# Moving the transposes of the next superblock's x into the first matmul, storing second-level results by whole rows, and pinning the order of matmuls and copies

## The chip, the cores and the metric

One core of one Trainium2 chip. The metric is the device time of one execution in microseconds (us).

## The reference

```python
x:  8 x 1024 x 1024 float32      w1: 1024 x 4096      w2: 4096 x 1024
h = x @ w1
h = 0.5 * h * (1 + np.tanh(np.sqrt(2 / np.pi) * (h + 0.044715 * h ** 3)))
return (h @ w2).astype(np.float32)
```

## The kernel before

The kernel works through eight superblocks (0 to 7) of 1024 rows of x. Each has a first matmul (x times w1, then the activation into `g`) and a second matmul (`g` times w2). Both use seven products of half-size blocks in place of eight (Strassen's scheme). In superblocks 2 to 7 some products of the second matmul are themselves split into seven smaller ones, with matmuls of 256 columns. These are the "inner" products, or the second level: 1, 2, 3, 6 and 7 in superblocks 3 to 7, and 2, 6 and 7 in superblock 2. The order of the products is 4, 1, 2, 3, 5, 6, 7. Superblocks 0 and 1 run code that the change does not touch.

Weights, operands and half results share one pool of 26 buffers named `u`. All loads, and the transposing DMAs, are issued by SP in one queue; casting and accumulating DMAs are issued by POOL.

```python
    up = ctx.enter_context(tc.tile_pool(name="up", bufs=26))
...
    def x_transpose(xb, dma):                    # 16 DMAs, x of one superblock, from the cast copy in DRAM
        blocks = x_blocks()                      # 4 buffers of the 26
        for b, t in blocks.items():
            a, k = int(b[0]) - 1, int(b[1]) - 1
            for j in range(KH):
                dma(t[:, j, :], xb[a * HT:(a + 1) * HT, (k * KH + j) * P:(k * KH + j + 1) * P],
                    transpose=True)
...
# first matmul, chunk c of 16: the next superblock's x is cast, late
            if 1 < sb < NSB - 1 and c in (8, 10, 12, 14):
                xb[0] = x_cast_paced(sb + 1, g["12"][:, c, :], c - 8, xb[0])
...
# an inner product: seven multiplies, each quarter of the result stored when it is done
            self.multiply(2, ab, False)
            ...
            self.done("11", c11)                 # store_quarter: rows of 256 float32, 1 KB
...
# second matmul
        def post5(q, ps):                        # product 5: first level, accumulates onto block 12
            store(sb, "12", q, copy(q, ps), accum_op=ADD)
            tt(u[q], u[q], ps, SUB, True)
            if not end:
                store(sb, "11", q, u[q])
...
        for m, after in zip(order, order[1:] + (None,)):
            if after is not None:
                load(after)                      # prefetch of the next product's weights
            if m == (1 if sb == 2 else 3):
                nxt[0] = next_x()                # the 16 transposes are issued here, on SP
...
```

The order of DVE's tensor operations in the second matmul is pinned to program order (`pin=True`). Matmuls and ACT's copies are placed by a scheduler when the kernel is built, and it interleaves neighbouring products.

Of the kernel before, what the change touches and what calls it, by code (L numbers as in the profile page):

```python
# [14 lines left out]
P = 128  # L15
# [75 lines left out]
def kernel(  # L91
# [14 lines left out]
    SB = 1024  # L106
# [47 lines left out]

    def load_in_order(out, in_, **kw):
        return tc.keep_in_program_order(nc.sync.dma_start(out=out, in_=in_, **kw))  # L156

    def pool_copy(out, in_):
        pool_last[0] = nc.gpsimd.tensor_copy(out=out, in_=in_)  # L159
# [180 lines left out]
        mark = nc.gpsimd.tensor_copy(out=pace, in_=g_chunk[:, :2])  # L340
        return x_cast(s, mark, range(q * P, (q + 2) * P, P), xb)

    def x_transpose(xb, dma):
        blocks = x_blocks()
        for b, t in blocks.items():
            a, k = int(b[0]) - 1, int(b[1]) - 1
            for j in range(KH):
                dma(  # L348
                    t[:, j, :],
                    xb[a * HT:(a + 1) * HT, (k * KH + j) * P:(k * KH + j + 1) * P],  # L350
                    transpose=True,
                )
        return blocks
# [3 lines left out]
    def matmul1(xs, sb, quads):  # L357
# [26 lines left out]
        more = []  # L384
        xb = [None]
        early = {1: {}, 2: {}}

        def ahead(q, step):

# [24 lines left out]
        for c in range(NI):  # L414
            q, j = divmod(c, QC)
            if sb > 1:
                if c % 2 == 0:
                    quads += [StoredHalf(i) for i in range(len(quads), min(c // 2 + 3, NI // 2))]
                w = quads[c // 2], c
            else:  # L420
                if j == 0:
                    ahead(q + 1, 0)
                w = quads[q], c
            pb, qb = psum(), psum()
            product(pb, w, 4, True, False)
            v = temp()
            nc.scalar.copy(out=v, in_=pb)  # L427
            product(qb, w, 5, True, False)
            u = temp()
            tt(u, v, qb, SUB)  # L430
            if late is not None:
                finish(*late)
            rb = psum()
            product(rb, w, 1, True, False)
            s = temp()
            tt(s, u, rb, ADD)
            if sb == 0 and c < 2:
                for m in SUMS:
                    quads[0].sum(m, more[c], True)
            product(pb, w, 2, False, True)  # L440
            gelu("21", c, pb)
            s2 = temp()
            tt(s2, s, pb, SUB)
            product(qb, w, 3, False, False)
            gelu("12", c, qb)
            product(rb, w, 7, False, True)
            c11 = temp()
            tt(c11, u, rb, ADD)
            gelu("11", c, c11)
            late = (c, w, qb, s2)  # L450
            if sb < 2 and j:
                ahead(q + 1, j)
            if 1 < sb < NSB - 1 and c in (8, 10, 12, 14):
                xb[0] = x_cast_paced(sb + 1, g["12"][:, c, :], c - 8, xb[0])
            if sb > 1 and c >= NI - 4:
                m, b = EARLY[c - NI + 4]
                if m in FILL_2[sb == 2]["inner"]:
                    early[m][b] = unit(NI // 2, HT // 2)
                    gu, gv = (inner_block(g[t], b) for t in A_TERMS[m])
                    nc.gpsimd.tensor_tensor(out=early[m][b], in0=gu, in1=gv, op=SUB)  # L460
        finish(*late)
        return g, xb[0], early



# [2 lines left out]
        o0 = (int(b[1]) - 1) * OH  # L468
        return nc.gpsimd.dma_start(out=out2[r0:r0 + P, o0:o0 + OH], in_=src, **kw)

    def store_quarter(sb, o, b, src, queue=None, add=None):
        add = queue is None if add is None else add
        queue = queue or nc.gpsimd
        r0 = sb * SB + (int(o[0]) - 1) * HT + (int(b[0]) - 1) * HT // 2
        o0 = (int(o[1]) - 1) * OH + (int(b[1]) - 1) * OH // 2
        rows = out2[r0:r0 + HT // 2, o0:o0 + OH // 2].rearrange("(i p) n -> p i n", p=P)
        return queue.dma_start(out=rows, in_=src, **(dict(accum_op=ADD) if add else {}))  # L477

    def matmul2_made(sb, g, keep_w1, xb):

# [135 lines left out]
                fill.pop(0)()  # L616
        while fill:
            fill.pop(0)()
        return at["last"], xs, [quad]

    def split_jobs(m, pieces):
        t = {}
# [32 lines left out]
    class Inner:  # L655


        def __init__(self, m, g, done=lambda b, t: None, base=None, x=()):
            self.m, self.done, self.base = m, done, base
            self.u, self.v = (None if b is None else g[b] for b in A_TERMS[m])  # L660
            self.x, self.s, self.y = dict(x), {}, {}
            if self.v is None:
                self.x = {b: inner_block(self.u, b) for b in BLOCKS}
# [16 lines left out]
        def multiply(self, j, bank, first):  # L680
            t = self.x[S_TERMS[j]] if j in S_TERMS else next(
                self.s[n] for n in S_SUMS if S_SUMS[n][0] == j
            )
            for i in range(2):
                for c in range(NI // 2):
                    nc.tensor.matmul(  # L686
                        bank[:, i * OH // 2:(i + 1) * OH // 2],
                        lhsT=t[:, c, i * P:(i + 1) * P],
                        rhs=self.y[j][:, c, :],
                        start=(first and i == 0 and c == 0),  # L690
                        stop=(c == NI // 2 - 1),
                        skip_group_check=not first or i > 0,
                    )

        def steps(self, into):

# [4 lines left out]
            ab, bb, cb = psum(), psum(), psum()  # L701
            self.multiply(1, ab, True)
            v = temp()
            nc.scalar.copy(out=v, in_=ab)
            yield 1
            self.multiply(6, bb, True)
            tt(c12, pair(v), pair(bb), ADD, True)
# [2 lines left out]
            yield 2  # L710
            self.multiply(2, ab, False)
            if base is None:
                nc.scalar.copy(out=c11, in_=pair(ab))
            else:
                tt(c11, b11, pair(ab), ADD, True)
            self.done("11", c11)
            yield 3
            self.multiply(7, bb, False)
            tt(c21, pair(v), pair(bb), ADD, True)
# [3 lines left out]
            yield 4  # L723
            self.multiply(5, cb, True)
            tt(c22, c21 if base is None else c22, pair(cb), ADD, True)
            self.done("22", c22)
            yield 5
            self.multiply(4, ab, True)
            tt(c21, c21, pair(ab), SUB, True)
            self.done("21", c21)  # L730
            yield 6
            self.multiply(3, cb, False)
            tt(c12, c12, pair(cb), ADD, True)
            self.done("12", c12)
            yield 7

    def operand2(g, m, q, pin=False):
# [6 lines left out]
        tt(a, g[u][:, :, cols], g[v][:, :, cols], SUB, pin)  # L744
        return a

    def matmuls2(bank, a, pieces, first, cs=range(NI)):
        for c in cs:
            nc.tensor.matmul(  # L749
                bank,  # L750
                lhsT=a[:, c, :],
                rhs=pieces[c // QC][:, c % QC, :],
# [1 line left out]
                stop=(c == NI - 1),  # L754
                skip_group_check=not first,
            )

    def product2(g, m, pieces, banks, first, by_chunk=False):
        if first:
# [13 lines left out]
        tiles = [up.tile([P, 2, OH], F32, name="u") for _ in range(2)]  # L773
        return tiles, [tiles[q // 2][:, q % 2, :] for q in range(NQ)]

    def matmul2(sb, g, early, next_x):
        inner = FILL_2[sb == 2]["inner"]
        fill = FILL_2[sb == 2]["fill"]
        end = sb == NSB - 1
        ops, pieces, splits = {}, {}, {}  # L780
        u2, u = halves()
        into, rows = {}, {}
        nxt = [None]

        products = {
            1: Inner(1, g, x=early[1]),
            2: Inner(2, g, lambda b, t: store_quarter(sb, "21", b, t), x=early[2]),
            3: Inner(3, g, lambda b, t: store_quarter(sb, "12", b, t, add=False)),
            6: Inner(6, g, lambda b, t: store_quarter(sb, "22", b, t)),
            7: Inner(  # L790
                7, g,
                lambda b, t: store_quarter(sb, "11", b, t, nc.sync if end else None),
                u2 if end else None,
            ),
        }

        def copy(q, ps):
            t = temp()
            nc.scalar.copy(out=t, in_=ps)
            return t  # L800

        def post4(q, ps):
            nc.scalar.copy(out=u[q], in_=ps)  # L803
            store(sb, "21", q, u[q])

        def post1(q, ps):
            nc.scalar.copy(out=rows[1][q], in_=ps)

        def post3(q, ps):
            d = rows[1][q]  # L810
# [18 lines left out]
        def run(key):  # L829
            for job in fill.get(key, ()):  # L830
# [13 lines left out]
                elif kind in "de":  # L844
                    b = job[1:]
                    d = quarter(into[1], b)
                    tt(d, d, quarter(into[2 if kind == "d" else 3], b), SUB if kind == "d" else ADD, True)
                    if kind == "e":
                        store_quarter(sb, "22", b, d, add=False)
                elif nxt[0] is not None:  # L850
                    nxt[0].make(m, pin=True)

        order = (4, 1, 2, 3, 5, 6, 7)
        load(4)
# [1 line left out]
        for m, after in zip(order, order[1:] + (None,)):  # L856
            if after is not None:
                load(after)
            if m == (1 if sb == 2 else 3):
                nxt[0] = next_x()  # L860
            if m in inner or m == 1:
                into[m], rows[m] = halves()
            if m in inner:
# [3 lines left out]
            for q in range(NQ):  # L867
                ps = psum()
                a = ops.get((m, q))
                matmuls2(ps, operand2(g, m, q) if a is None else a, pieces[m], True)  # L870
                posts[m](q, ps)
                run((m, q))
        return nxt[0]

    idle = consts.tile([P, HT], DT, name="idle")
    nc.vector.memset(idle, 0.0)
# [3 lines left out]
    nc.scalar.activation(out=warm, in_=warm, func=GELU)  # L880
    xs, quads = x_first(), []
    for sb in range(NSB):
        g, xb, early = matmul1(xs, sb, quads)
        if sb < 2:
            xb = x_cast(sb + 1, quads[2].stored) if sb else None
            last, xs, quads = matmul2_made(sb, g, None if sb else quads[-1].keep_raw, xb)
            continue
        def next_x():
            return XOps(x_transpose(xb, nc.sync.dma_start)) if xb is not None else None

        xs = matmul2(sb, g, early, next_x)
        if xs is not None:
            quads = [StoredHalf(0)]


# [28 lines left out]
```

## Time and profile before

| | before |
|---|---|
| time, median of the first 3 runs | 1576.93 us (1576.26 to 1580.64) |
| span of the profiled run | 1578.6 us |
| PE busy | 1531.9 us, 97% |
| superblock 2 | 205.2 us |
| superblocks 3 to 6 | 189.5, 195.6, 192.8, 192.5 us |
| superblock 7, to the end of the last matmul | 190.5 us |

A superblock is measured in PE's timeline, from the first matmul of 512 columns of its first matmul to that of the next one. What it needs can be worked out from durations in the same timeline. Sixteen 512-column matmuls in a row start 0.216 us apart, sixteen 256-column ones take 1.75 us (0.1094 each). So superblocks 3 to 7 need 448 x 0.216 + 128 x 0.216 + 560 x 0.1094 = 185.7 us, and superblock 2, with fewer inner products, 448 x 0.216 + 256 x 0.216 + 336 x 0.1094 = 188.8 us (the recorded texts say 188.9).

From the page of the kernel before, the line of the engines (busy us, share of the span, instructions):

```profile
PE 1531.9 (97%) x8606; PEld 839.5 (53%) x8606; DVE 1066.9 (68%) x1354; ACT 486.2 (31%) x821; POOL 387.2 (25%) x434
```

From the list of who waited for whom, PE's largest waits (total us, times, longest):

```profile
PE ps L686 <- DVE u L146: 11.9, 5, 10.3
PE ps L686 <- DMA u<-in_d: 11.8, 11, 2.0
PE ps L686 <- ACT tmp L704: 4.3, 6, 0.7
PE ps L686 <- DVE gc L146: 3.3, 6, 1.4
PE ps L364 <- DMA u<-w_d: 3.3, 9, 0.5
```

PE is 97% busy, so everything that can be won is a wait of PE, and the waits are short and many. L686 is the inner products' matmul; `in_d` holds their weights.

Three stretches of superblock 4 (us, then busy time and instruction count of PE, PEld, DVE, ACT, POOL, then PE's clock, the busy share of the DMAs, GB/s). The first lies in the first matmul, the other two in the second:

```profile
852.00:858.00 6.00, 6.00 (x29) 2.74 (x28) 3.40 (x6) 2.88 (x6) 1.30 (x1) 1.00 0.01 3
...
942.00:948.00 6.00, 6.00 (x56) 5.37 (x57) 6.00 (x9) 0.58 (x1) 3.80 (x4) 1.00 1.28 131
948.00:954.00 6.00, 5.82 (x45) 4.24 (x44) 5.14 (x8) 0.00 (x0) 0.92 (x2) 1.00 1.45 128
```

SP's timeline (start, us, engine, line, operation, count) and PE's (the bracket is the idle time before, and what ended it) in the same superblock:

```profile
933.12 26.81 SPq L348 DMA_TRANSPOSE u<-xb  x16
960.03 18.34 SPq L668 DMA_DIRECT2D u<-in_d  x14
```

```profile
975.42 1.92 PE L686 MATMUL ps<-u,gc 128*128 128x256 f16 x16 [1.96 <-DMA u<-in_d]
...
991.99 3.65 PE L686 MATMUL ps<-u,gc 128*128 128x256 f16 x32 [1.07 <-DMA u<-in_d]
```

Read together: in the first matmul the DMAs stand nearly idle at 852 us. In the second their busy share is above 1 at 942 to 954 us and yet they move only about 130 GB/s, while the 16 transposes run there. The loads of `in_d` are issued after them, and PE's waits for them end 15 to 32 us later. The time from issue to landing of these 14 loads:

```profile
DMA to landing us min/median/max: 5.8/17.2/19.6
```

Superblock 2 has one long wait. The chain of waits there (start, us, what):

```profile
581.41 14.35 DMA out_dram<-u
...
596.99 1.23 DVE u L146
```

PE's timeline at its end:

```profile
598.27 3.53 PE L686 MATMUL ps<-u 128*128 128x256 f16 x16 [10.29 <-DVE u L146]
```

DVE waited for a buffer that a store had to empty, and the store took 14.35 us to land. The 16 matmuls after the gap take 3.53 us, where others take 1.91 us. The Trainium skill ("TensorE: Matmul & The Clock Gate", Part 1) says that PE falls to half its clock after about 3.4 us of idleness and needs about 3.4 us of work to come back. This wait agrees: the clock column is 1.00 from 588 to 590 us, 0.50 from 592 to 600 us, and 1.00 again from 602 us.

### The profile page before, as it was taken

Reading aid. Unit: us, or ns where it says so; the run is one execution under the profiler, and the core shown is the slowest. Engines: PE = TensorE matmul, PEld = TensorE weight load, DVE = VectorE, ACT = ScalarE, POOL = GpSimd, SP = SyncE. Lnnn points to the kernel's source line nnn. Section 1 sums busy time; section 2 is a strip of 40 time slices with the busy share of each in tenths; the row PEclk is TensorE's granted clock in tenths of the full one; section 3 lists DMA queues with packets and bytes.
Section 4 is the critical chain, followed back from the end, with each engine's and each line's share of the span. In section 5 each row is a group of like instructions: output and inputs, shape, how many; then the busy total and the mean of one; then the engine's idle time right before and its main releaser. Section 6 shows DMA issues by size and latency. Waiting matters only on the chain.

```text
span 1578.6 us, 22771 instructions
## 1 busy us (share of the span) xinstructions
PE 1531.9 (97%) x8606; PEld 839.5 (53%) x8606; DVE 1066.9 (68%) x1354; ACT 486.2 (31%) x821; POOL 387.2 (25%) x434
## 2 busy tenths in 40 slices
PE   9999999999999988999999998999999999999998
PEld 4444444444444545447754476544765448644486
DVE  6876867879656557555865668656686566855577
ACT  6654024400344112441124411344113431144311
POOL 2341011223121332130422213131131401404022
PEclk9999999999999998999999999999999999999999
DMA  9999976985947999569995799957999579993597
GB/s 321 338 339 337 260 244 226 307 262 214 386 145 205 269 360 274 203 168 319 277 328 199 210 270 297 338 169 217 260 313 333 164 222 247 334 342 116 200 312 196
DMA packets 222221, 415.19 MB, mean 263 GB/s; under 512 B 78240, under 2 KB 102816, under 8 KB 221216
## 3 DMA queue, kind: packets, MB, share of 16 engines
q1 hardware_dynamic: 178560, 307.29, 58.7%
q0 software_dynamic: 43552, 106.45, 27.0%
q8 instruction: 67, 1.10, 0.3%
q14 instruction: 42, 0.34, 0.1%
HBM read 304.09 MB, written 124.26 MB: 271 GB/s over the span
## 4 chain that ended last, share of the span: by engine, by line
PE 75%; DMA 14%; DVE 4%; issue 4%; SPq 1%; ACT 1%; POOL 1%; POOLq 0%; DVEq 0%
PE ps L364 46%; PE ps L749 20%; PE ps L686 9%; DMA u<-in_d 6%; DMA u<-w_d 3%; DMA out_dram<-u 3%; DVE u L146 3%; DMA gc<-in_w_dram 2%; DVE gc L146 1%; DMA in_d<-u 1%; SPq L156 1%; DMA out_dram<-tmp 1%; ACT u L803 0%; SPq L348 0%; POOL u L159 0%
## 5 line engine op out<-in xcount | busy, mean ns | idle before, releaser
L364 PE MATMUL ps<-u 128*128 128x512 f16 x3584 | 778.2, 380 | 6.8 <-DMA u<-w_d 3.3
L364 PEld LDWEIGHTS <-u 128*128 128x128 f16 x3584 | 349.1, 98 | 433.8 <-DMA u<-w_d 8.5
L146 DVE TENSOR_TENSOR tmp<-tmp,ps 128x512 f32<-128x512 f32 x528 | 362.2, 687 | 299.1 <-ACT tmp L427 113.5
L374 ACT ACTIVATE g<-tmp 128x512 f16<-128x512 f32 x256 | 161.2, 630 | 294.7 <-DVE tmp L146 294.6
L749 PE MATMUL ps<-u,gc 128*128 128x512 f16 x1088 | 237.4, 380 | 0.0
L146 DVE TENSOR_TENSOR u<-u 128x2048 f16<-128x2048 f16 (+3 forms) x245 | 219.0, 923 | 18.2 <-ACT u L319 12.2
L686 PE MATMUL ps<-u,gc 128*128 128x256 f16 x1792 | 210.8, 273 | 9.1 <-DMA u<-in_d 5.6
L686 PEld LDWEIGHTS <-gc 128*128 128x128 f16 x1792 | 174.1, 98 | 36.8 <-issue 9.0
L374 ACT ACTIVATE g<-ps 128x512 f16<-128x512 f32 x256 | 151.4, 596 | 91.6 <-PE ps L364 90.6
L749 PEld LDWEIGHTS <-gc 128*128 128x128 f16 x1088 | 106.4, 98 | 126.3
L477 POOL DMA_DIRECT2D out_dram<-u x108 | 111.5, 1033 | 246.6 <-DVE u L146 183.2
L460 POOL TENSOR_TENSOR u<-g,g 128x2048 f16<-128x2048 f16 x22 | 89.1, 4072 | 296.9 <-ACT g L374 296.9
L686 PE MATMUL ps<-u 128*128 128x256 f16 x1104 | 136.4, 275 | 23.4 <-DVE u L146 11.2
L749 PE MATMUL ps<-u,g 128*128 128x512 f16 x704 | 154.2, 380 | 1.7 <-DMA u<-w_d 1.7
L686 PEld LDWEIGHTS <-u 128*128 128x128 f16 x1104 | 107.8, 98 | 43.8 <-DVE u L146 17.0
L749 PEld LDWEIGHTS <-g 128*128 128x128 f16 x704 | 68.9, 98 | 83.9 <-issue 1.5
L146 DVE TENSOR_TENSOR u<-tmp,ps 128x512 f32<-128x512 f32 x56 | 38.4, 686 | 109.4 <-PE ps L686 72.0
L146 DVE TENSOR_TENSOR u<-u,ps 128x512 f32<-128x512 f32 x129 | 88.1, 683 | 28.6 <-PE ps L749 17.1
L146 DVE TENSOR_TENSOR u<-g,g 128x2048 f16<-128x2048 f16 x70 | 83.5, 1220 | 19.6 <-DMA out_dram<-u 11.1
L427 ACT COPY tmp<-ps 128x512 f32<-128x512 f32 x128 | 72.9, 569 | 73.8 <-PE ps L364 73.6
L146 DVE TENSOR_TENSOR tmp<-ps,tmp 128x512 f32<-128x512 f32 x128 | 88.4, 691 | 6.4 <-PE ps L364 1.6
L146 DVE TENSOR_TENSOR gc<-g,g 128x2048 f16<-128x2048 f16 x68 | 82.3, 1219 | 3.0 <-PE ps L749 1.6
(43 smaller groups left out, 547.1 us busy)
## 6 DMA issues: line engine op xcount, KB each, us to landing
u<-in_d SPq DMA_DIRECT2D x196, 512.0 KB, 7.8
u<-w_d SPq DMA_DIRECT2D x240, 256.0 KB, 5.4
out_dram<-u POOLq DMA_DIRECT2D x164, 256.0 KB, 8.2
u<-raw_d SPq DMA_DIRECT2D x56, 512.0 KB, 7.1
gc<-in_w_dram SPq DMA_DIRECT2D x48, 512.0 KB, 6.1
u<-raw_d SPq DMA_DIRECT2D x96, 256.0 KB, 5.4
raw_d<-u SPq DMA_DIRECT2D x32, 512.0 KB, 9.8
w_d<-u POOLq DMA_DIRECT2D x32, 512.0 KB, 4.3
```

What stands on the lines that cost most here:

```text
L146: i = nc.vector.tensor_tensor(out=out, in0=in0, in1=in1, op=op)
L156: return tc.keep_in_program_order(nc.sync.dma_start(out=out, in_=in_, **kw))
L364: nc.tensor.matmul(bank, lhsT=ops[:, k, :], rhs=xs[m][:, k, :], start=(first and k == 0), stop=(k == KH - 1), skip_group_check=not first,)
L374: gelu_last[0] = nc.scalar.activation(out=g[b][:, c, :], in_=src, func=GELU)
L427: nc.scalar.copy(out=v, in_=pb)
L460: nc.gpsimd.tensor_tensor(out=early[m][b], in0=gu, in1=gv, op=SUB)
L477: return queue.dma_start(out=rows, in_=src, **(dict(accum_op=ADD) if add else {}))
L686: nc.tensor.matmul(bank[:, i * OH // 2:(i + 1) * OH // 2], lhsT=t[:, c, i * P:(i + 1) * P], rhs=self.y[j][:, c, :], start=(first and i == ...
L749: nc.tensor.matmul(bank, lhsT=a[:, c, :], rhs=pieces[c // QC][:, c % QC, :], start=(first and c == 0), stop=(c == NI - 1), skip_group_chec ...
```

## The change

The intent is to move the traffic for the next superblock's x out of the second matmul, to make the stores' rows longer, and to keep the products in the order in which they were written.

```diff
-            if 1 < sb < NSB - 1 and c in (8, 10, 12, 14):
-                xb[0] = x_cast_paced(sb + 1, g["12"][:, c, :], c - 8, xb[0])
+            if 1 < sb < NSB - 1:
+                if c in (1, 3, 5, 7):
+                    xb[0] = x_cast_paced(sb + 1, g["12"][:, c, :], c - 1, xb[0])
+                if c == 9:
+                    blocks = x_blocks()
+                if c > 8 and c % 2:
+                    x_transpose(xb[0], load_in_order, blocks, range((c - 9) // 2, (c - 7) // 2))
...
-            if m == (1 if sb == 2 else 3):
-                nxt[0] = next_x()
...
+    def store_rows(sb, o, a, src, **kw):
+        r0 = sb * SB + (int(o[0]) - 1) * HT + a * HT // 2
+        o0 = (int(o[1]) - 1) * OH
+        rows = out2[r0:r0 + HT // 2, o0:o0 + OH].rearrange("(i p) n -> p i n", p=P)
+        return nc.gpsimd.dma_start(out=rows, in_=src, **kw)
...
-            3: Inner(3, g, lambda b, t: store_quarter(sb, "12", b, t, add=False)),
+            3: Inner(3, g, out("12")),           # out: store_rows, called when both quarters of a row are done
...
+    def act_copy(out, in_):
+        tc.keep_in_program_order(nc.scalar.copy(out=out, in_=in_))
...
-                    nc.tensor.matmul(             # inner products; likewise in matmuls2
+                    tc.keep_in_program_order(nc.tensor.matmul(
```

The three parts are called X (early casts and transposes of x), R (rows of 2 KB) and P (pins) from here on.

More of the change, by code (lines that the diff above doesn't have):

```diff
@@ L341, in x_cast_paced, with x_transpose @@
         return x_cast(s, mark, range(q * P, (q + 2) * P, P), xb)
-    def x_transpose(xb, dma):
-        blocks = x_blocks()
-        for b, t in blocks.items():
+    def x_transpose(xb, dma, blocks=None, which=range(4)):
+        blocks = blocks or x_blocks()
+        for b, t in [list(blocks.items())[i] for i in which]:
             a, k = int(b[0]) - 1, int(b[1]) - 1
@@ L386, in matmul1 @@
         early = {1: {}, 2: {}}
+        blocks = None
         def ahead(q, step):
@@ L461, in matmul1 @@
         finish(*late)
-        return g, xb[0], early
+        return g, early, None if blocks is None else XOps(blocks)
     def store(sb, b, q, src, **kw):
@@ L469, in store, with store_quarter @@
         return nc.gpsimd.dma_start(out=out2[r0:r0 + P, o0:o0 + OH], in_=src, **kw)
-    def store_quarter(sb, o, b, src, queue=None, add=None):
-        add = queue is None if add is None else add
-        queue = queue or nc.gpsimd
+    def store_quarter(sb, o, b, src):
         r0 = sb * SB + (int(o[0]) - 1) * HT + (int(b[0]) - 1) * HT // 2
@@ L476, in store_quarter @@
         rows = out2[r0:r0 + HT // 2, o0:o0 + OH // 2].rearrange("(i p) n -> p i n", p=P)
-        return queue.dma_start(out=rows, in_=src, **(dict(accum_op=ADD) if add else {}))
+        return nc.sync.dma_start(out=rows, in_=src)
+    def store_rows(sb, o, a, src, **kw):
[3 more added lines that the diff above has]
+        return nc.gpsimd.dma_start(out=rows, in_=src, **kw)
     def matmul2_made(sb, g, keep_w1, xb):
@@ L618, in matmul2_made @@
             fill.pop(0)()
-        return at["last"], xs, [quad]
+        return xs, [quad]
     def split_jobs(m, pieces):
@@ L655, with __init__ @@
     class Inner:
-        def __init__(self, m, g, done=lambda b, t: None, base=None, x=()):
-            self.m, self.done, self.base = m, done, base
+        def __init__(self, m, g, rows=lambda a, t: None, part=lambda b, t: None, base=None, x=()):
+            self.m, self.rows, self.part, self.base = m, rows, part, base
             self.u, self.v = (None if b is None else g[b] for b in A_TERMS[m])
@@ L692, in multiply @@
                         skip_group_check=not first or i > 0,
-                    )
+                    ))
         def steps(self, into):
@@ L703, in steps @@
             v = temp()
-            nc.scalar.copy(out=v, in_=ab)
+            act_copy(v, ab)
             yield 1
@@ L712, in steps @@
             if base is None:
-                nc.scalar.copy(out=c11, in_=pair(ab))
+                act_copy(c11, pair(ab))
             else:
                 tt(c11, b11, pair(ab), ADD, True)
-            self.done("11", c11)
+            self.part("11", c11)
             yield 3
@@ L725, in steps @@
             tt(c22, c21 if base is None else c22, pair(cb), ADD, True)
-            self.done("22", c22)
+            self.part("22", c22)
             yield 5
@@ L729, in steps @@
             tt(c21, c21, pair(ab), SUB, True)
-            self.done("21", c21)
+            self.part("21", c21)
+            self.rows(1, into[1])
             yield 6
@@ L733, in steps @@
             tt(c12, c12, pair(cb), ADD, True)
-            self.done("12", c12)
+            self.part("12", c12)
+            self.rows(0, into[0])
             yield 7
@@ L745, in operand2, with matmuls2 @@
         return a
-    def matmuls2(bank, a, pieces, first, cs=range(NI)):
+    def matmuls2(bank, a, pieces, first, cs=range(NI), pin=False):
         for c in cs:
-            nc.tensor.matmul(
+            i = nc.tensor.matmul(
                 bank,
@@ L756, in matmuls2 @@
             )
+            if pin:
+                tc.keep_in_program_order(i)
     def product2(g, m, pieces, banks, first, by_chunk=False):
@@ L774, in halves, with matmul2 @@
         return tiles, [tiles[q // 2][:, q % 2, :] for q in range(NQ)]
-    def matmul2(sb, g, early, next_x):
+    def matmul2(sb, g, early, nxt):
         inner = FILL_2[sb == 2]["inner"]
@@ L782, in matmul2, with out @@
         into, rows = {}, {}
-        nxt = [None]
+        def out(o, **kw):
+            return lambda a, t: store_rows(sb, o, a, t, **kw)
         products = {
             1: Inner(1, g, x=early[1]),
-            2: Inner(2, g, lambda b, t: store_quarter(sb, "21", b, t), x=early[2]),
-            3: Inner(3, g, lambda b, t: store_quarter(sb, "12", b, t, add=False)),
-            6: Inner(6, g, lambda b, t: store_quarter(sb, "22", b, t)),
-            7: Inner(
-                7, g,
-                lambda b, t: store_quarter(sb, "11", b, t, nc.sync if end else None),
-                u2 if end else None,
-            ),
-        }
+            2: Inner(2, g, out("21", accum_op=ADD), x=early[2]),
+            3: Inner(3, g, out("12")),
+            6: Inner(6, g, out("22", accum_op=ADD)),
+        }
+        if end:
+            products[7] = Inner(7, g, part=lambda b, t: store_quarter(sb, "11", b, t), base=u2)
+        else:
+            products[7] = Inner(7, g, out("11", accum_op=ADD))
         def copy(q, ps):
             t = temp()
-            nc.scalar.copy(out=t, in_=ps)
+            act_copy(t, ps)
             return t
         def post4(q, ps):
-            nc.scalar.copy(out=u[q], in_=ps)
+            act_copy(u[q], ps)
             store(sb, "21", q, u[q])
         def post1(q, ps):
-            nc.scalar.copy(out=rows[1][q], in_=ps)
+            act_copy(rows[1][q], ps)
         def post3(q, ps):
@@ L847, in run @@
                     tt(d, d, quarter(into[2 if kind == "d" else 3], b), SUB if kind == "d" else ADD, True)
-                    if kind == "e":
-                        store_quarter(sb, "22", b, d, add=False)
-                elif nxt[0] is not None:
-                    nxt[0].make(m, pin=True)
+                    if job in ("e21", "e12"):
+                        a = int(b[0]) - 1
+                        store_rows(sb, "22", a, into[1][a])
+                elif nxt is not None:
+                    nxt.make(m, pin=True)
         order = (4, 1, 2, 3, 5, 6, 7)
@@ L869, in matmul2 @@
                 a = ops.get((m, q))
-                matmuls2(ps, operand2(g, m, q) if a is None else a, pieces[m], True)
+                matmuls2(ps, operand2(g, m, q) if a is None else a, pieces[m], True, pin=True)
                 posts[m](q, ps)
                 run((m, q))
-        return nxt[0]
     idle = consts.tile([P, HT], DT, name="idle")
@@ L882 @@
     for sb in range(NSB):
-        g, xb, early = matmul1(xs, sb, quads)
+        g, early, nxt = matmul1(xs, sb, quads)
         if sb < 2:
             xb = x_cast(sb + 1, quads[2].stored) if sb else None
-            last, xs, quads = matmul2_made(sb, g, None if sb else quads[-1].keep_raw, xb)
+            xs, quads = matmul2_made(sb, g, None if sb else quads[-1].keep_raw, xb)
             continue
-        def next_x():
-            return XOps(x_transpose(xb, nc.sync.dma_start)) if xb is not None else None
-        xs = matmul2(sb, g, early, next_x)
-        if xs is not None:
-            quads = [StoredHalf(0)]
+        matmul2(sb, g, early, nxt)
+        if nxt is not None:
+            xs, quads = nxt, [StoredHalf(0)]
 _INS = ['x', 'w1', 'w2']
```

## The prediction

> **What bounds it now.** The first block shows PE busy 97% of 1578.6 us, so only PE's stalls can be won. The list of who waited for whom adds up to about 41 us of PE waits; the large ones are 11.9 us for tiles made by DVE (one of 10.3), 11.8 us for u<-in_d loads, 5.0 us for u<-w_d loads, 4.3 us for an ACT copy and 3.3 us for DVE sums. From PE's timeline: a full matmul takes 0.216 us, one of 256 columns 0.1094 us (16 take 1.75 us). Superblocks 3 to 6 therefore need 448 x 0.216 + 128 x 0.216 + 560 x 0.1094 = 185.7 us of PE. They take 189.4, 195.6, 192.8 and 192.5 us, so 27.5 us are lost in the four. Superblock 2 needs 188.9 and takes 205.2 (16.3 lost, 10.3 of it one wait at 588 us, after which the clock drops to 0.5); superblock 7 loses about 8, half of it the tail. Superblocks 0 and 1 are untouched.
>
> **Why they stall.** Stretches of 6 us in superblock 4: in the first matmul the DMAs are full until 846 us, then nearly idle (0.01 to 0.25) for some 20 us. In the second they are full from 925 us to the end. The 16 x transposes are issued there, over 27 us (1.3 us each), with only 99 to 166 GB/s moving against about 340 without them. The in_d loads stand behind them on SP's queue: issue starts at 960, PE waits for them at 973 to 992 us.
>
> **What the change does.** DVE's order does not change at all; PE's and ACT's do, and PE has the same matmuls. It
> 1. moves 16 transposes (about 20 us of DMA) into the idle stretch, for superblocks 2 to 6, and the casts 40 us earlier;
> 2. halves the second-level stores to 512 KB each (1 KB rows become 2 KB);
> 3. pins PE to program order, so that products no longer interleave; the 0.72 (ACT) and 0.39 (DVE) waits of each superblock should go, since every operand is made one or more products ahead.
> The Trainium skill ("DMA: Bandwidth & Descriptors", SWDGE vs HWDGE vs iDMA) says that all issuing engines share the same 16 DMA engines; this trace agrees (transposes cut the total to 99 GB/s), which is why moving them helps loads and stores alike.
>
> Price: x of the next superblock holds four more of 26 buffers through the second matmul. I traced the reuse: in steady state each load's buffer still comes free 14 to 25 us of PE time ahead of its use, against landings of 8 us.
>
> **Sum.** Superblocks 3 to 6: 27.5 lost becomes about 8 (-19). Superblock 2: the operand that DVE waited for still needs a buffer that an accumulating store empties (that store took 14.35 us to land), so only -8. Superblock 7: -2. Together -29: **1548 us**, range 1537 to 1567. Faster by over 2%: 0.40; within 2%: 0.58; slower: 0.02.
>
> **Checks.** Right if: superblocks 3 to 6 take 186 to 188.5 us each; PE's wait for u<-in_d falls from 11.8 to under 3 us; transposes start about 55 us into the first matmul with DMA busy there; the 10.3 us wait shrinks to 3 to 6 us; ACT waits of 0.72 disappear.
>
> **What would make it wrong.** Transposes and casts in the first matmul delay w_d loads or the first w2 pieces (PE waits at the start of the second matmul); program order exposes DVE sums, which are back to back there (5.5 to 6 us busy in 6.1); stores of 512 KB hold their buffers longer; superblock 2's wait stays whole or vanishes.

## More of the kernel before

A "round" runs a kernel and the kernel before on the same chip, one after the other.

```profile
DMA to landing us min/median/max: 3.8/6.0/8.6
```

The loads land late, the stores beside the transposes do not.

## The result, and the profile after

The changed kernel took 1540.4 us in the median of 4 runs (1538.5 to 1540.98), against 1577.3 us of 4 runs of the kernel before. The ratio is 0.976 (95% interval 0.9743 to 0.9778). A ratio here is the mean time of one kernel's fast runs over that of the other's fast runs of the same rounds, so it is not quite the ratio of the medians.

| | before | after |
|---|---|---|
| span of the profiled run | 1578.6 us | 1538.1 us |
| PE busy | 97% | 99% |
| superblock 2 | 205.2 us | 196.2 us |
| superblocks 3 to 6 | 189.5, 195.6, 192.8, 192.5 us | 185.8 us, four times |
| superblock 7, to the last matmul | 190.5 us | 185.9 us |

The profiled run of the kernel before was its slowest, so the two profiles lie 40.5 us apart and the medians 36.9 us.

The line of the engines, after:

```profile
PE 1523.8 (99%) x8606; PEld 844.5 (55%) x8606; DVE 1071.2 (70%) x1354; ACT 489.3 (32%) x821; POOL 330.7 (21%) x380
```

All waits of PE above 1 us in sum, after:

```profile
PE ps L699 <- DVE u L146: 4.0, 7, 2.3
PE ps L699 <- DVE gc L146: 2.1, 1, 2.1
PE ps L367 <- DVE tmp L146: 1.7, 5, 0.5
PE ps L296 <- DVE warm L895: 1.2, 1, 1.2
PE ps L367 <- DVE u L146: 1.1, 1, 1.1
```

No wait for a load is left. Stretches of superblock 4, which now begins at 791.1 us; the first three lie in the first matmul, the last in the second:

```profile
834.00:840.00 6.00, 6.00 (x29) 2.74 (x28) 3.44 (x5) 2.88 (x6) 1.10 (x3) 1.00 0.00 0
...
846.00:852.00 6.00, 6.00 (x30) 2.70 (x29) 3.44 (x5) 2.89 (x6) 3.68 (x2) 1.00 0.56 135
...
864.00:870.00 6.00, 6.00 (x29) 2.74 (x28) 3.44 (x5) 2.89 (x6) 0.00 (x0) 1.00 0.52 93
...
929.00:935.00 6.00, 6.00 (x57) 5.37 (x55) 3.90 (x6) 0.59 (x1) 0.00 (x0) 1.00 1.00 258
```

SP's and PE's timelines there:

```profile
844.30 5.04 SPq L156 DMA_TRANSPOSE u<-xb  x4
...
852.91 15.59 SPq L156 DMA_TRANSPOSE u<-xb  x12
868.60 2.49 SPq L270 DMA_DIRECT2D u<-w_d  x4
...
924.50 36.93 SPq L681 DMA_DIRECT2D u<-in_d  x14
```

```profile
957.65 3.65 PE L699 MATMUL ps<-u,gc 128*128 128x256 f16 x32 [0.16 <-DVE u L146]
```

SP issues the transposes for 20.6 us in the first matmul. The DMAs are 0.51 to 0.68 busy there, but 0.99 (285 GB/s) from 852 to 858 us, where loads of weights land too. The 14 `in_d` loads are issued from 924.50 us, which is 133.4 us after the superblock's start, where it was 156.6 us before (960.03 less 803.4). Their issue is spread over 36.93 us and each lands soon:

```profile
DMA to landing us min/median/max: 4.2/6.0/8.3
```

The 0.16 us is the only wait of PE shown in this superblock.

What is left sits in superblock 2 (PE's timeline, then the chain of waits):

```profile
577.37 1.92 PE L699 MATMUL ps<-u,gc 128*128 128x256 f16 x16 [2.08 <-DVE gc L146]
...
581.97 3.65 PE L699 MATMUL ps<-u,gc 128*128 128x256 f16 x32 [0.93 <-DVE u L146]
...
589.68 2.78 PE L699 MATMUL ps<-u,gc 128*128 128x256 f16 x16 [2.31 <-DVE u L146]
```

```profile
554.45 14.74 DMA out_dram<-u
...
574.74 10.10 DMA out_dram<-u
```

The chain still leads through the landing of two stores. After the first landing (569.19 us) DVE works without a pause until the wait at 577 us ends.

The 32 matmuls that begin at 589.68 us take 5.16 us to the start of the next, where others take 3.50 us: the clock fell here too.

```profile
591.00:593.00 2.00, 2.00 (x11) 1.45 (x10) 2.00 (x3) 0.00 (x0) 1.23 (x1) 0.50 0.82 322
```

The column is 1.00 up to 590.5 us and again from 594 us. So the three waits (5.32 us) and the half clock (1.66 us) are together 7.0 of the 7.4 us that superblock 2 takes beyond its 188.8 us. PE had waited only 2.31 us, less than the 3.4 us cited above. Whether a wait of this length brings the fall differs from kernel to kernel: in superblock 2 it followed waits of 2.31 us (here), 2.60 us (rows_not3) and 2.79 us (no_pins), but not waits of 2.71 us (only_x) and 2.67 us (pe_pins):

```profile
589.95 1.91 PE L699 MATMUL ps<-u,gc 128*128 128x256 f16 x16 [2.67 <-DVE u L146]
```

Times of superblock 2 that differ by 1 or 2 us must be read with this in mind.

### The profile page after: what moved, and what is told of

The parts are those of the page before. It is cut to its first block, busy times and chain, and to the rows that moved or that the text cites. A ratio compares the mean times of both kernels' runs of the same rounds, so it can differ in the third digit from the quotient of the medians.

```text
span 1538.1 us, 22679 instructions
## 1 busy us (share of the span) xinstructions
PE 1523.8 (99%) x8606; PEld 844.5 (55%) x8606; DVE 1071.2 (70%) x1354; ACT 489.3 (32%) x821; POOL 330.7 (21%) x380
## 2 busy tenths in 40 slices
DMA packets 212654, 415.19 MB, mean 270 GB/s; under 512 B 77376, under 2 KB 84544, under 8 KB 211648
## 4 chain that ended last, share of the span: by engine, by line
PE 90%; DMA 5%; DVE 2%; issue 1%; SPq 1%; ACT 0%; POOL 0%; DVEq 0%; POOLq 0%; ACTq 0%
PE ps L367 48%; PE ps L764 22%; PE ps L699 20%; DMA out_dram<-u 2%; DMA gc<-in_w_dram 2%; DVE u L146 1%; SPq L156 1%; DVE gc L146 1%; DMA u<-in_d 0%; DVE tmp L146 0%; DMA u<-in_x_dram 0%; ACT u L181 0%; POOL u L162 0%; ACT g L377 0%; POOL out_dram L478 0%
## 5 line engine op out<-in xcount | busy, mean ns | idle before, releaser
L699 PE MATMUL ps<-u 128*128 128x256 f16 x1104 | 132.6, 274 | 0.0
L159 ACT COPY tmp<-ps 128x512 f32<-128x512 f32 x56 | 32.8, 586 | 274.0 <-PE ps L699 151.8
L490 POOL DMA_DIRECT2D out_dram<-u x54 | 55.6, 1038 | 282.4 <-DVE u L146 263.3
L431 ACT COPY tmp<-ps 128x512 f32<-128x512 f32 x128 | 72.9, 570 | 70.4 <-PE ps L367 69.7
L478 POOL DMA_DIRECT2D out_dram<-u x56 | 41.2, 764 | 240.8 <-ACT u L159 212.2
```

What stands on the lines that cost most here:

```text
L159: tc.keep_in_program_order(nc.scalar.copy(out=out, in_=in_))
L431: nc.scalar.copy(out=v, in_=pb)
L478: return nc.gpsimd.dma_start(out=out2[r0:r0 + P, o0:o0 + OH], in_=src, **kw)
L490: return nc.gpsimd.dma_start(out=rows, in_=src, **kw)
L699: tc.keep_in_program_order(nc.tensor.matmul(bank[:, i * OH // 2:(i + 1) * OH // 2], lhsT=t[:, c, i * P:(i + 1) * P], rhs=self.y[j][:, c, : ...
```

## The experiments

The theory was that the transposes, in a second matmul whose DMAs were already full, caused most of the loss (T). The rivals were that program order caused most of the gain (P), or the row size (S). Each of the three parts was switched alone and in pairs. Times are medians of 4 or 5 runs; ratios are to the kernel before in the same rounds.

| parts | run | us | ratio | superblock 2 | superblocks 3 to 6 |
|---|---|---|---|---|---|
| none | before | 1576 to 1579 | 1 | 205.2 | 189.5 to 195.6 |
| X | only_x | 1550.5 | 0.984 | 193.5 | 188.4 |
| R | only_rows | 1587.7 | 1.008 | 203.3 | 194.3 to 196.2 |
| P | only_pins | 1572.3 | 0.998 | 200.2 | 185.8, then 192.9 to 194.4 |
| X+R | no_pins | 1575.7 | 0.999 | 194.6 | 194.1 to 196.4 |
| X+P | no_rows | 1540.8 | 0.976 | 197.3 | 185.8 |
| R+P | no_x | 1567.1 | 0.994 | 201.4 | 189.5 to 193.0 |
| X+R+P | after | 1540.4 | 0.976 | 196.2 | 185.8 |

### X alone: only_x

Edit: the first two hunks of the diff alone, with quarter stores and without pins.

> The kernel before with one part of the change alone: casts and transposes of x in the first matmul (1 KB store rows and unpinned order as before). Theory T (the transposes in the crowded second matmul are the main cause): nearly all of the 37 us comes back, 1548 to 1555 us; PE's waits for in_d loads vanish; the 0.72 and 0.39 us waits of each superblock stay. Rival P (program order is the main cause): under 10 us of gain, 1567 us or more. Rival S (small store rows are the main cause): under 10 us of gain, and the 10 us wait of superblock 2 stays.

Measured: 1550.5 us, ratio 0.9839 (0.9824 to 0.9853). The gain is two thirds of the whole, so T holds and both rivals fall as main causes. It is less than "nearly all of the 37 us", though. PE's waits in superblock 4:

```profile
910.26 2.12 PE L699 MATMUL ps<-u 128*128 128x256 f16 x18 [0.72 <-ACT tmp L159]
...
916.05 5.42 PE L699 MATMUL ps<-u,gc 128*128 128x256 f16 x48 [0.39 <-DVE gc L146]
...
934.16 1.91 PE L699 MATMUL ps<-u,gc 128*128 128x256 f16 x16 [0.23 <-DVE u L146]
...
965.83 1.91 PE L699 MATMUL ps<-u,gc 128*128 128x256 f16 x16 [0.22 <-DVE u L146]
```

The waits for loads are gone. The waits of the interleaved order stay, and each superblock takes 188.4 us: 2.6 us more than with pins, of which these brackets show 1.56 us. A matmul's end is modelled in the profile (16 that take 1.75 us in a row show as 1.91 us), so a bracket is somewhat too short.

### R alone: only_rows

Edit: the `store_rows` hunks alone.

> The kernel before with the 2 KB store rows alone. Theory T: 2 to 5 us of gain, 1572 to 1575 us, nearly all of it in superblock 2. Rival P: the same. Rival S: 15 us or more, 1562 us or less.

Measured: 1587.7 us, ratio 1.0078 (1.0061 to 1.0095). Every theory missed this: it is a loss of 12 us. Superblock 4 has one long wait, and the chain before it is the one that is taken up under no_pins.

```profile
984.72 3.57 PE L695 MATMUL ps<-u,gc 128*128 128x256 f16 x16 [5.86 <-DVE u L146]
```

### P alone: only_pins

Edit: `keep_in_program_order` around the matmuls and ACT's copies alone.

> The kernel before with matmuls and copies pinned to program order alone. Theory T: 4 to 7 us of gain (the 1.1 us of ACT and DVE waits in each of six superblocks), 1570 to 1573 us; DMA waits of the second matmul stay near 5 us in superblocks 4 to 6. Rival P: 20 us or more. Rival S: nothing, or 4 us.

Measured: 1572.3 us, ratio 0.9975 (0.996 to 0.999), which is a little less than T expected. The waits for `in_d` did not stay: the list of waits shows that they moved to the first weights of the next superblock.

```profile
PE ps L367 <- DMA u<-w_d: 13.4, 8, 3.8
...
PE ps L695 <- DMA u<-in_d: 1.6, 6, 0.5
```

Superblock 3 already takes 185.8 us here, with its x still transposed late; superblocks 4 to 6 pay at their start. Late loads are the limit, and the order only decides at which product PE meets them.

### The change without X: no_x

Edit: the first two hunks undone.

> The changed kernel with x cast late and transposed in the second matmul again (rows and pins kept). Theory T: it gives back 20 to 30 us, 1562 to 1570 us, with waits for in_d loads back in superblocks 3 to 6. Rival P and rival S: at most 8 us given back, 1548 us or less.

Measured: 1567.1 us, ratio 0.994 (0.9924 to 0.9957), 26.7 us above the changed kernel: T holds. The waits are back, as expected:

```profile
PE ps L695 <- DMA u<-in_d: 17.3, 27, 1.4
```

### Casts or transposes: casts_early

```diff
                 if c in (1, 3, 5, 7):
                     xb[0] = x_cast_paced(sb + 1, g["12"][:, c, :], c - 1, xb[0])
-                if c == 9:
-                    blocks = x_blocks()
-                if c > 8 and c % 2:
-                    x_transpose(xb[0], load_in_order, blocks, range((c - 9) // 2, (c - 7) // 2))
...
+            if m == (1 if sb == 2 else 3) and next_xb is not None:
+                nxt[0] = XOps(x_transpose(next_xb, nc.sync.dma_start))
```

> The changed kernel with only the casts early; the 16 transposes are back in the second matmul. If the transposes are what hurts there: as the kernel with both late, 1562 to 1571 us, waits for in_d loads back. If the late casts were the harm (their traffic in the last third of the first matmul): 1548 us or less.

Measured: 1565.8 us, ratio 0.992 (0.9904 to 0.9937), 1.3 us below no_x, with intervals that overlap. The waits for loads are back:

```profile
PE ps L695 <- DMA u<-in_d: 16.0, 24, 1.2
```

Early casts are only what makes early transposes possible; the place of the transposes, in time and in SP's queue, is worth the 25 us.

### The change without R: no_rows

Edit: `out("12")` and the others store by quarters of 1 KB rows on POOL again.

> The changed kernel with second-level results stored by quarters of 1 KB rows again (early x and pins kept). Theory T2 (rows matter only through superblock 2, and there they may cost rather than help, since the x-only kernel had no loss there): superblocks 3 to 6 stay at 185.8 us, superblock 2 takes 193 to 198 us, in all 1538 to 1543 us. Rival S (stores of 2 KB rows carry part of the steady gain): superblocks 3 to 6 at 188 us or more, in all 1549 us or more.

Measured: 1540.8 us, ratio 0.976 (0.9743 to 0.9777), the same as the changed kernel. With early x and pins the row size is worth nothing that these runs can see. Superblock 2 takes 197.3 us with quarters and 196.2 us with rows, in one profile of each.

### The change without P: no_pins

Edit: both pins off.

> The changed kernel with matmuls and copies left to the scheduler again (early x and rows kept). T2: the interleaved products cost 2.6 us in each of superblocks 3 to 6 as in the x-only kernel (188.4 us), and rows add a wait for a store as in the rows-only kernel: 1550 to 1560 us. Rival (the pins matter only where x is late): 1545 us or less.

Measured: 1575.7 us, ratio 0.9986 (0.9968 to 1.0004). The rival falls, and the loss was larger than expected: without pins, rows undo the whole gain of X. Each of superblocks 3 to 6 has one long wait. The chain of waits leads to the one of superblock 4, and PE's timeline (second block) shows it:

```profile
951.32 10.27 DMA out_dram<-u
...
963.29 10.47 DMA out_dram<-u
...
975.00 0.69 DVE u L146
```

```profile
975.73 3.57 PE L699 MATMUL ps<-u,gc 128*128 128x256 f16 x16 [6.18 <-DVE u L146]
```

The wait is followed by half clock here too (the 16 matmuls after it take 3.57 us). The store issued at 951.32 us is product 3's first rows of block 12. POOL's next store of product 5 accumulates onto the same rows and must wait for that landing, and POOL issues in order. So the store of product 5's half result behind it leaves at 963.29 us and lands 10.47 us later. DVE's operand for product 7 was given that half result's buffer, and PE waits for DVE. Stored by quarters, the first quarter leaves earlier: in POOL's timeline of only_x the pause before the first accumulating store of product 5 is 4.1 us, here it is 8.1 us.

### Product 3 by quarters, all else as in no_pins: rows_not3

```diff
-            3: Inner(3, g, out("12")),
+            3: Inner(3, g, part=lambda b, t: store_quarter(sb, "12", b, t, nc.gpsimd)),
```

> The unpinned kernel with early x and row stores, but product 3's result by quarters again. Theory W (without pins, the row store of product 3 is issued late, POOL's next store accumulates onto the same rows and waits in order for its landing, the stores behind it come late, and DVE waits 6 to 9 us for the buffer that one of them empties): superblocks 3 to 6 fall from 195 to about 188.4 us, in all 1548 to 1554 us. Rival (row stores are bad in themselves, or another product's): 1565 us or more.

Measured: 1551.4 us, ratio 0.9834 (0.9819 to 0.9849), superblocks 188.4 us: as only_x. So product 3's row store is the one that hurts. One reservation: in this build DVE's operand also got another buffer, one that a matmul empties. Which of the two links of the chain alone would have been enough is open.

### Which pins: pe_pins

Edit: `act_copy` calls a plain `nc.scalar.copy`; matmuls stay pinned.

> The changed kernel with only the matmuls pinned, ACT's copies left to the scheduler. ACT has the same copies in nearly the same order, so if the matmuls' order is what counts: 1539 to 1542 us. If the copies' pins carry part of it: 1545 us or more.

Measured: 1539.7 us, ratio 0.9759 (0.9742 to 0.9776). The pins on the matmuls carry all of it.

### What holds superblock 2: sb2_quarters, sb2_act, sb2_base

sb2_quarters stores by quarters in superblock 2 alone.

> The changed kernel with quarter stores in superblock 2 alone. If the row stores cause superblock 2's remaining 7 us (196.2 against 193.5 in the x-only kernel, needed 188.9): superblock 2 at 193 us or less and 1537 us or less. If the pinned order does: superblock 2 at 195 to 197 us and 1539 to 1541 us.

Measured: 1540.0 us, ratio 0.9755 (0.9739 to 0.9771); superblock 2 takes 196.2 us. Row stores are not what holds it. The alternative, that the pinned order does, foresaw 195 to 197 us and 1539 to 1541 us, and it fits: from no_pins to the changed kernel, which differ in the pins alone and both have a clock fall, superblock 2 goes from 194.6 to 196.2 us, in one profile of each. So the pins, which win 2.6 us in each of superblocks 3 to 6, seem to cost about 1.6 us here.

sb2_act issues superblock 2's plain stores of products 3 and 5 from ACT:

```diff
-            store(sb, "12", q, copy(q, ps))
+            store(sb, "12", q, copy(q, ps), nc.scalar)
...
-                store(sb, "11", q, u[q])
+                store(sb, "11", q, u[q], nc.scalar if sb == 2 else None)
```

> The changed kernel with superblock 2's twelve plain first-level stores of products 3 and 5 issued by ACT instead of POOL, so that they don't stand behind POOL's other stores. If superblock 2's last 7 us come from late stores in POOL's order: superblock 2 falls from 196.2 to 190 to 192 us, in all 1534 to 1537 us. If landing itself is slow because the DMAs are full: superblock 2 stays at 195 us or more, 1539 to 1541 us.

Measured: 1540.0 us, ratio 0.9762 (0.9746 to 0.9778); superblock 2 takes 196.1 us. The wait only changed its place (chain of waits, then PE's timeline):

```profile
560.37 14.55 DMA out_dram<-u
```

```profile
579.07 3.60 PE L699 MATMUL ps<-u,gc 128*128 128x256 f16 x16 [4.51 <-DVE gc L146]
```

A store issued by ACT takes 14.55 us to land, as POOL's did. The DMA share is 1.03 to 1.08 in every 10 us from 540 to 590 us. The Trainium skill ("DMA: Bandwidth & Descriptors", SWDGE vs HWDGE vs iDMA) says that issuing from several engines saves only the sequencer's time to issue, since all of them feed the same 16 DMA engines. This run agrees.

sb2_base takes traffic away instead: in superblock 2 product 5 does not store its half of block 11, and product 7 adds it on the core.

```diff
+        elif sb == 2:
+            products[7] = Inner(7, g, out("11"), base=u2)
...
-            if not end:
+            if not end and sb != 2:
                 store(sb, "11", q, u[q])
```

> The changed kernel; in superblock 2 product 5 no longer stores its half of block 11: product 7 adds it on the core, as the last superblock does, and stores rows without accumulation. [...]DVE's operands for product 7 come to lie in buffers that matmuls empty, not stores. If late landings of stores in full DMAs are the cause of the last 7 us of superblock 2: the wait of 2 to 4 us near 587 us goes, the one near 577 us stays (its buffer still hangs on a store of product 3), superblock 2 takes 191 to 193.5 us, in all 1534.5 to 1537.5 us. If something else holds it: 196 us and 1539 to 1541 us.

Measured: 1537.8 us (1537.23 to 1539.04), ratio 0.9746 (0.9733 to 0.9759); superblock 2 takes 193.5 us. PE's waits there:

```profile
577.14 1.92 PE L699 MATMUL ps<-u,gc 128*128 128x256 f16 x16 [2.08 <-DVE gc L146]
581.73 3.65 PE L699 MATMUL ps<-u,gc 128*128 128x256 f16 x32 [0.93 <-DVE u L146]
...
600.58 1.91 PE L699 MATMUL ps<-u,gc 128*128 128x256 f16 x16 [1.22 <-DVE u L146]
```

The 2.31 us wait at 589 us is gone and the one at 577 us stays, as expected; the total is 0.3 us above the expected range. This was the lowest median. Its gain over the changed kernel is 2.8 us in the trace of superblock 2: 2.31 us of wait and 1.66 us of half clock are gone (the clock column stays at 1.00), and a new wait of 1.22 us at 600 us has come. The two ratios come from different rounds and their intervals overlap, so the times alone do not separate the two. The page of this run counts 1.05 MB less moved by the DMAs than that of the changed kernel (414.14 against 415.19 MB). The edit both takes traffic away and gives DVE's operands other buffers; which of the two counts was not separated.

## Why the prediction was right

The measured 1540.4 us lies in the range of 1537 to 1567 us, 7.6 us below the predicted 1548 us. The chance was put at 0.40 for faster by over 2%, and it was faster by 2.4%; the prediction held "within 2%" (0.58) more likely. The sizes of the superblocks below are differences of the two profiles; their sum, 40.8 us, is larger than the 36.9 us between the medians, because the profile before is of that kernel's slowest run.

- *The cause.* "Transposes in the second matmul, in_d loads behind them" was right: no_x and casts_early give back 25 to 27 us, and X alone brings 25 us. Whether the loads suffered from standing behind the transposes in SP's queue, or from the DMA engines being full, was not separated by an experiment. The traces speak for the queue: the loads were issued only after the last transpose and then landed together, a median of 17.2 us after issue (6.0 us in the changed kernel), while the stores that POOL issued beside the transposes took a median of 6.0 us. "Helps loads and stores alike" is therefore not shown for stores.
- *Superblocks 3 to 6, predicted -19 us, measured -27.2 us* (770.4 less 4 x 185.8). This was the term that was mis-sized. I left 8 us of waits in place as a margin, without any wait to name for them. The count of needed PE time (185.7 us) was already the answer: 185.8 us was reached. My check "186 to 188.5 us each" had its lower edge too high.
- *Superblock 2, predicted -8 us, measured -9.0 us.* Right in size, and nearly for the reason given: its chain of waits still hangs on stores that take 10.1 and 14.7 us to land. They are not accumulating stores, as the prediction says, and neither was the one of 14.35 us: the kernel accumulates first-level results from `tmp` alone, and these are `out_dram<-u`. Where I expected one wait of 3 to 6 us, there are three of 2.08, 0.93 and 2.31 us, and 1.66 us of half clock, for which the sum had no term.
- *Superblock 7, predicted -2 us, measured -4.6 us* to the last matmul (190.5 to 185.9). Again the margin was unfounded.
- *The pins.* The prediction gave them 1.1 us of each superblock, by the two brackets. With X they are worth 2.6 us of each (188.4 to 185.8) and 9.7 us in all (only_x to no_rows), since superblock 2 loses some of it. Without X they are worth only about 4 us, because PE then meets the late loads elsewhere.
- *The rows.* The prediction listed them and gave them no number, and beside X and P they are worth none (no_rows). What it did not see is that rows without pins cost 12 us alone and 25 us beside X. The parts of this change do not add up, so its sum by parts could not have given the effect of any part of it. That the total held all the same was luck in this respect: with X and rows but without pins (no_pins, 1575.7 us) it would have missed its range.
- *The price.* Four more buffers held through the second matmul cost nothing visible in superblocks 3 to 7. The slack of 14 to 25 us that I found by following the reuse of buffers was enough. Program order did not expose DVE's sums, but for 0.16 us.

## What to carry to other kernels

When PE is nearly always busy, first work out from the trace what each stage needs at full rate, then look at which stretch has full DMAs and which has idle ones. Moving traffic that is not urgent from the full stretch to the idle one, and out of the queue in front of urgent loads, was worth more here than anything done about the stores. A longer row or a larger transfer leaves later, and if something accumulates onto it from the same in-order queue, the delay is passed on: test such a part alone and together with the others.

## What the Trainium skill lacked or had wrong

- "DMA: Bandwidth & Descriptors" (Latency and other measured facts) gives DMA transposes an effective 261 GB/s, and about 350 to 400 GB/s when contiguous. Here SP issued 16 transposes of 128 KB in 20.6 us (2.1 MB, about 102 GB/s), with the DMAs 0.51 to 0.68 busy for most of it. SP spends 1.26 us (median) on issuing each, and one follows the other, so its issue and not the DMAs set the pace: these runs do not show the page's figure wrong, only that a program may not come near it.
- The same page has no figure for ordinary traffic beside transposes. Here stretches of the second matmul fell to 128 to 131 GB/s at a DMA share of 1.28 to 1.45, where a like stretch without transposes moved 258 GB/s at 1.00. SP issued no loads in these stretches, and POOL's stores there landed in 3.8 to 8.6 us, so it is not shown that the transposes slowed other transfers.
- No page that I used tells how long a store takes to land while the DMAs are full. For the stores in the chains shown it was 10.1 to 14.7 us for 256 KB to DRAM, from POOL and from ACT alike, and that latency, passed on through a reused buffer, is where the chain of the last waits of superblock 2 leads.
